# First group's 32x32 solve on VectorE, the bias table in four parts, up projections on GpSimd's queue

## The chip, the cores and the metric

The kernel runs on one core of one Trainium2 chip. A core has TensorE (PE in the profile: matmuls, with PEld for its weight loads), VectorE (DVE), ScalarE (ACT), GpSimd (POOL) and SyncE (SP, which here only issues DMAs). Each engine works through its own instructions in a fixed order and waits on semaphores; DMAs are issued from the queues of SyncE, ScalarE and GpSimd. The metric is the device time of one execution in microseconds. Before the change the median of three runs is 2808.73 us (2807.68 to 2812.29).

## The reference

Two transformer blocks of 256 tokens and width 2048, one after the other, all in float32. The change concerns only the first half of the first block:

```python
def first_block(x, ...):
    u = rms_norm(x, norm1_g)
    proj = u @ w_in                       # 2048 x 6432
    q, k, v, z = split(proj, ...)
    attn = dilated_attention(q, k, v, rel_bias_table)   # 16 heads of 64
    rw = rwkv7_time_mix(z, ...)                         # 16 heads of 64
    h = x + concat([attn, rw]) @ w_out
    h = h + (silu(gate) * up) @ w_down    # feed-forward, 5632
    return rms_norm(h, final_g)

def rwkv7_step(state, inp):               # scanned over the 256 tokens
    r, w, k, v, a, bb = inp
    sa = einsum('bhij,bhj->bhi', state, a)
    state = state * w + sa * bb + v * k   # outer products per head
    return state, einsum('bhij,bhj->bhi', state, r)

def reference(x, ...):
    return second_block(first_block(x, ...), mem_2, ...)
```

The attention's bias depends on the distance of query and key alone: `bias_table[t5_bucket(...)]`, 32 buckets by 16 heads. The second block (three attentions, a gated merge, a convolution and a feed-forward) is left as it is.

## The kernel before

Every large product is a call of `lin` (lines 344 to 399). A weight matrix lies packed in blocks of up to 512 columns; for each pair of k-tiles SyncE loads a `raw` tile (line 376), ScalarE rounds it to `wh` (line 385), VectorE subtracts to get the rest `wl` (line 386), and TensorE runs three matmuls for each k-tile and each half of the tokens (line 394): high by high, high by low, low by high. The tiles come from rings, three `raw`, three `wh`, two `wl`, and after the first block a second ring is made on the memory that its tiles give up. So TensorE can be ahead of VectorE and ScalarE by a few tiles only.

`block1_mix` runs the projections of the first block in a fixed list and, between their k-tiles, a set of tasks written as generators: `tick` adds the matmuls' modelled nanoseconds to a program clock and steps each task whose due time has come; a `yield 4000.0` puts the task to sleep for so much of that clock. The program order that results is the order in which each engine gets its instructions, except that weight loads and splits are pulled ahead by a priority (`LOAD_AHEAD`, `SPLIT_AHEAD`). The tasks are:

- `rwkv`: for each of four groups of four heads, `rwkv_pre` and `rwkv_group`. The scan over tokens is done in chunks of 32, eight in a group. `rwkv_group` makes the 32x32 blocks D of all chunks (VectorE masks them, line 621), stores them with two DMAs to `scN` (line 626), transposes v into UV, and calls `solve_T`. That loads N back from `scN` (four DMAs, line 654), loads an identity into T (line 657), and inverts the triangular blocks by 31 steps of a multiplication (line 662) and an addition (line 664), 62 small operations, each of which needs the one ahead of it. T goes to `scT` (line 666).
- `chains`: for each group the recurrence over eight chunks, from `load_solved` (T back as `TTx`, line 674) through `chain`: in each chunk matmuls `ch` on TensorE (line 727), with small copies on VectorE and ScalarE between them (`Xc`, `UV`, `Ux`, `S`, `Y`, lines 699 to 721). After a chain `rwkv_out` does the group norm (lines 735 to 743), a transpose `yt`, the gate `g` and the scaling `rw`, and splits the result into `mixh` and `mixl`.
- `attention`: quarters of four heads; `attn_load` brings `L`, the bias of two heads at a time laid out by query and key (line 883), q, k and v.

The bias comes from `attn_consts`: a matmul looks up all distances, VectorE copies the row `brow`, GpSimd stores it to `biasd` (line 786) and two DMAs write the table `toepd` (16 heads x 128 x 384) from it with a shifted start for each query (line 791). `load_up` loads the up projections `lup` of a group with two DMAs (line 521).

The last projection of the block is w_out in four blocks of 512 columns. As long as tasks are left, `block1_mix` runs passes over its first 14 of 16 k-tiles into spools `wa`; `block1_out` then does the blocks without a pass in full, and the rest with the last two k-tiles, adding `wa`.

## Time and profile before

| | before |
|---|---|
| median of three runs | 2808.73 us |
| profiled execution | 2810.79 us |
| its span, first to last instruction | 2808.8 us |
| mean granted TensorE clock | 0.996 |
| TensorE busy | 2763.9 us, 98% |
| VectorE busy | 1741.4 us, 62% |
| ScalarE busy | 1551.5 us, 55% |
| GpSimd busy | 167.2 us, 6% |
| HBM read | 518.46 MB |

A row of a timeline reads: start in us, duration in us, engine, line, operation, what it writes and reads, how often, and in brackets the idle time of the engine ahead of it and what ended it. A row of the windows has each engine's busy time with its count of instructions, then the granted clock, the share of time in which the DMA engines were busy, and GB/s. A row of the waits has the total, the number and the longest. Lines are those of the kernel before. Buffer numbers are left out of names.

### The profile page before, as it was taken

The page shows a single profiled execution, that of the slowest core. Times are in us where ns is not written, and L with a number is a line of the kernel's source. Part 1 is how long each engine was busy: PE and PEld are TensorE (multiplying, and loading weights), DVE is VectorE, ACT ScalarE, POOL GpSimd, SP SyncE. Part 2 cuts the span into 40 slices and gives each one's busy share as a digit, 9 for nine tenths or more (in the row PEclk, how much of TensorE's full clock was granted, in tenths as well). Part 3 has the DMA queues.
Part 4 walks back from the last instruction along what each step waited for, and adds up shares of the span by engine and source line. Part 5 has one row for each costly group of instructions (what it writes and reads, how often), then busy time and mean ns, then how long its engine had stood idle before and what let it go on. Part 6 is the DMA issues. An engine that isn't in the chain of part 4 may idle for free.

```text
span 2808.8 us, 40012 instructions
## 1 busy us (share of the span) xinstructions
PE 2763.9 (98%) x13496; PEld 2313.9 (82%) x13496; DVE 1741.4 (62%) x3121; ACT 1551.5 (55%) x2847; POOL 167.2 (6%) x380
## 2 busy tenths in 40 slices
PE   7989999999999999999999999999999999999999
PEld 7878888878888888888888888888888888888887
DVE  5666777675555555555756666665667676766554
ACT  6545556555455454444655755555556666666444
POOL 2432404000000000000000000000000000000000
PEclk9999999999999999999999999999999999999999
DMA  8555557766666666666754556666555555555665
GB/s 250 183 160 183 187 177 220 229 200 186 189 192 188 189 190 191 188 192 190 222 184 155 161 175 200 200 201 196 186 187 185 187 180 187 186 185 186 202 201 166
DMA packets 163910, 534.76 MB, mean 190 GB/s; under 512 B 18993, under 2 KB 29879, under 8 KB 163704
## 3 DMA queue, kind: packets, MB, share of 16 engines
q1 hardware_dynamic: 149644, 503.24, 57.0%
q10 hardware_dynamic: 9516, 16.27, 1.7%
q0 software_dynamic: 4544, 12.69, 1.6%
q8 instruction: 106, 1.74, 0.3%
q14 instruction: 100, 0.82, 0.1%
HBM read 518.46 MB, written 16.82 MB: 191 GB/s over the span
## 4 chain that ended last, share of the span: by engine, by line
PE 91%; DMA 4%; POOL 2%; DVE 1%; ACT 1%; issue 1%; SPq 0%; DVEq 0%; ACTq 0%; POOLq 0%
PE lin L394 84%; PE ch L727 2%; PE tr L263 1%; DMA toepd<-biasd 1%; PE uT L263 1%; POOL T L664 1%; DVE wl L386 1%; POOL X L662 0%; PE D L257 0%; PE o L257 0%; DMA raw<-in_w_in_dram 0%; ACT wh L385 0%; PE pt L257 0%; PE lg L257 0%; ACT junk L293 0%
## 5 line engine op out<-in xcount | busy, mean ns | idle before, releaser
L386 DVE TENSOR_TENSOR wl<-raw,wh 128x512 fp32r<-128x512 f32 (+2 forms) x1848 | 1267.4, 688 | 853.3 <-PE lin L394 758.2
L385 ACT CAST wh<-raw 128x512 fp32r<-128x512 f32 (+2 forms) x1848 | 1140.1, 619 | 1080.5 <-PE lin L394 1014.1
L394 PE MATMUL lin<-wl,x2h 128*128 128x512 f32 (+2 forms) x800 | 295.0, 369 | 3.8 <-DVE wl L386 3.8
L394 PE MATMUL lin<-wh,x2l 128*128 128x512 f32 (+2 forms) x800 | 291.2, 365 | 0.0
L394 PE MATMUL lin<-wl,u2h 128*128 128x512 f32 x704 | 281.0, 399 | 0.0
L394 PE MATMUL lin<-wl,hhi 128*128 128x512 f32 x704 | 275.0, 391 | 0.0
L394 PE MATMUL lin<-wh,u2l 128*128 128x512 f32 x704 | 274.6, 390 | 0.0
L394 PE MATMUL lin<-wl,uh 128*128 128x512 f32 x704 | 274.0, 391 | 0.0
L394 PE MATMUL lin<-wh,hlo 128*128 128x512 f32 x704 | 274.0, 389 | 0.0
L394 PE MATMUL lin<-wh,ul 128*128 128x512 f32 x704 | 272.3, 390 | 0.6 <-DVE ul L330 0.6
L394 PE MATMUL lin<-wh,x2h 128*128 128x512 f32 (+2 forms) x800 | 248.1, 366 | 0.1
L394 PE MATMUL lin<-wh,uh 128*128 128x512 f32 x704 | 228.1, 391 | 0.6 <-ACT uh L329 0.6
L394 PE MATMUL lin<-wh,u2h 128*128 128x512 f32 x704 | 225.5, 392 | 0.0
L394 PE MATMUL lin<-wh,hhi 128*128 128x512 f32 x704 | 220.0, 389 | 0.0
L394 PE MATMUL lin<-wl,xh 128*128 128x512 f32 (+2 forms) x512 | 192.2, 376 | 6.6 <-DVE wl L386 6.4
L394 PE MATMUL lin<-wh,xl 128*128 128x512 f32 (+2 forms) x512 | 178.5, 349 | 0.0
L394 PEld LDWEIGHTS lin<-wl,x2h 128*128 128x128 f32 x800 | 151.2, 189 | 30.2 <-DVE wl L386 7.2
L394 PEld LDWEIGHTS lin<-wh,x2h 128*128 128x128 f32 x800 | 149.9, 189 | 25.4 <-ACT wh L385 1.2
L394 PEld LDWEIGHTS lin<-wh,x2l 128*128 128x128 f32 x800 | 151.2, 189 | 22.9
L394 PE MATMUL lin<-wh,xh 128*128 128x512 f32 (+2 forms) x512 | 156.6, 354 | 11.7 <-ACT wh L385 11.7
L394 PEld LDWEIGHTS lin<-wh,uh 128*128 128x128 f32 x704 | 132.1, 188 | 28.7 <-ACT uh L329 1.5
L394 PEld LDWEIGHTS lin<-wh,u2h 128*128 128x128 f32 x704 | 132.1, 188 | 28.0
(426 smaller groups left out, 3735.6 us busy)
## 6 DMA issues: line engine op xcount, KB each, us to landing
raw<-in_w_in_dram SPq DMA_DIRECT2D x268, 512.0 KB, 3.7
raw<-in_w_gate_up_dram SPq DMA_DIRECT2D x176, 512.0 KB, 3.9
raw<-in_w_down_dram SPq DMA_DIRECT2D x176, 512.0 KB, 3.6
raw<-in_w_up_dram SPq DMA_DIRECT2D x176, 512.0 KB, 3.8
raw<-in_w_out_dram SPq DMA_DIRECT2D x64, 512.0 KB, 3.8
raw<-in_w_mem_kv_dram SPq DMA_DIRECT2D x16, 512.0 KB, 4.3
raw<-in_w_br_fox_dram SPq DMA_DIRECT2D x12, 512.0 KB, 4.3
raw<-in_w_br_sb_dram SPq DMA_DIRECT2D x12, 512.0 KB, 4.4
```

The costliest lines, as they stand in the source:

```text
L263: self.nc.tensor.transpose(out, in_, self.ident[p0:p0 + n, p0:p0 + n])
L385: nc.scalar.copy(wh[:, :m * n], raw[:, cs])
L386: nc.vector.tensor_tensor(wl[:, :m * n], raw[:, cs], wh[:, :m * n].bitcast(F32), op=ALU.subtract)
L394: self.nc.tensor.matmul(ps[tb], lhsT=x, rhs=w, start=k == first and i == 0 and not (one and tb), stop=k == last - 1 and i == 2, skip_group ...
L664: gp.tensor_tensor(w, w, x, op=ALU.add)
L727: self.nc.tensor.matmul(out, lhsT=lhsT, rhs=rhs, start=start, stop=True, skip_group_check=True)
```

## The change

The 62 operations of group 0's solve go from GpSimd to VectorE; groups 1 to 3 keep GpSimd. The loads of N and of the identity move into `load_N`, called right behind the two stores of D; the transposes of v come after them, and the solve is put into the program 13 us of program clock behind the loads. Since VectorE's weight splits can be pulled ahead of it by their priority, `hold` makes a 1x1 copy from the latest `wl` into a tile, which ties the tile's first use to that place among the weights. The time at which a solve counts as done becomes the clock plus 48 us (30 us for group 0).

The table is made in four tensors of four heads, each with its own hold, store and two writes, 10 us of program clock apart, and the task starts after block 4 of w_in instead of ahead of it. `lup` of groups 1 to 3 is loaded from GpSimd's queue.

```diff
--- before.py
+++ after.py
@@ -386,6 +386,7 @@
                     nc.vector.tensor_tensor(wl[:, :m * n], raw[:, cs], wh[:, :m * n].bitcast(F32), op=ALU.subtract)
                 for tb in range(2):
                     for j in range(m):
+                        self.at = wl
                         k = k0 + j0 + j
                         kx = k if kmap is None else kmap(k)
                         h, l = (t[:, j * n:(j + 1) * n] for t in (wh, wl))
@@ -401,6 +402,10 @@
 
     SPLIT_AHEAD = 0
     LOAD_AHEAD = 500
+
+    def hold(self, t):
+
+        self.nc.vector.tensor_copy(t, self.at[t.base_partition():t.base_partition() + 1, 0:1].bitcast(F32))
 
 
 class Block1(Builder):
@@ -518,7 +523,7 @@
         nc, cs = self.nc, slice(S * g, S * g + S)
         for i in range(2):
             r = slice(64 * i, 64 * i + 64)
-            nc.sync.dma_start(self.lup[r, i, :], self.A["lup"][r, cs])
+            (nc.gpsimd if g else nc.sync).dma_start(self.lup[r, i, :], self.A["lup"][r, cs])
 
     def rwkv_pre(self, g):
 
@@ -602,13 +607,6 @@
                 r = slice(64 * hh, 64 * hh + 64)
                 o = 64 * x + 32 * hh
                 v.tensor_tensor(BK[r, :, o:o + 32], c32(src)[r], st.linv[r], op=ALU.mult)
-        yield 1500.0
-        yield from wait("v")
-        st.v = self.mixed_T(nat[2], 2, st, self.slot([P, 2, S], "v"))
-
-        for p in range(2):
-            v.scalar_tensor_tensor(r_[:, p, :], r_[:, p, :], self.pv("r_k", 2 * st.g + p), k[:, p, :],
-                                   op0=ALU.mult, op1=ALU.mult)
         yield 4500.0
         st.D, st.BKT, st.UV = self.set2("D", [P, 16, P]), self.set2("BKT", [P, 16, P]), self.set2("UV", [P, 16, 64])
         for p in range(2):
@@ -625,6 +623,14 @@
         for hh in range(2):
             nc.gpsimd.dma_start(self.scN[hh].rearrange("c t s -> t c s"),
                                 st.D[32 * hh:32 * hh + 32, :, 32 * hh:32 * hh + 32])
+        self.load_N(st)
+        yield from wait("v")
+        st.v = self.mixed_T(nat[2], 2, st, self.slot([P, 2, S], "v"))
+
+        for p in range(2):
+            v.scalar_tensor_tensor(r_[:, p, :], r_[:, p, :], self.pv("r_k", 2 * st.g + p), k[:, p, :],
+                                   op0=ALU.mult, op1=ALU.mult)
+        yield 3000.0
         nc.gpsimd.memset(st.UV[0:64], 0.0)
         pv = self.aux("V")
         for i in range(4):
@@ -637,11 +643,22 @@
                     v.tensor_copy(dst, src[:, hh])
                 else:
                     nc.scalar.copy(dst, src[:, hh])
-        self.solve_T(st)
         yield 1300.0
         ps = self.aux("bn")
         self.mm(ps, self.same, r_.rearrange("p a s -> p (a s)"))
         v.tensor_tensor(r_, st.v, ps.rearrange("p (a s) -> p a s", a=2), op=ALU.mult)
+        yield max(0.0, st.sent + 13000.0 - self.clock)
+        self.solve_T(st)
+
+    def load_N(self, st):
+
+        gp = self.nc.gpsimd
+        st.N = self.p1.tile([P, 32, 32], F32, tag="N", name=self.nm("N"))
+        for q in range(4):
+            gp.dma_start(st.N[32 * q:32 * q + 32], self.scN.rearrange("h c t s -> (h c) t s"))
+        st.T = self.p1.tile([P, 8, 32], F32, tag="T", name=self.nm("T"))
+        gp.dma_start(st.T, self.A["c_eye4"].rearrange("p (a b) -> p a b", a=8))
+        st.sent = self.clock
 
     def solve_T(self, st):
 
@@ -649,23 +666,21 @@
 
         nc = self.nc
         gp = nc.gpsimd
-        N = self.p1.tile([P, 32, 32], F32, tag="N", name=self.nm("N"))
-        for q in range(4):
-            gp.dma_start(N[32 * q:32 * q + 32], self.scN.rearrange("h c t s -> (h c) t s"))
-        T = self.p1.tile([P, 8, 32], F32, tag="T", name=self.nm("T"))
+        N, T = st.N, st.T
         X = self.p1.tile([P, 256], F32, tag="X", name=self.nm("X"))
-        gp.dma_start(T, self.A["c_eye4"].rearrange("p (a b) -> p a b", a=8))
+        eng = gp if st.g else nc.vector
+        if not st.g:
+            self.hold(X[0:1, 0:1])
         for u in range(31):
             m, n = u // 4 + 1, 31 - u
             x = X[:, :m * n].rearrange("p (a b) -> p a b", a=m)
             w = T[:, 0:m, u + 1:32]
-            gp.tensor_tensor(x, T[:, 0:m, u:u + 1].to_broadcast([P, m, n]),
-                             N[:, u:u + 1, u + 1:32].to_broadcast([P, m, n]), op=ALU.mult)
-            gp.tensor_tensor(w, w, x, op=ALU.add)
+            eng.tensor_tensor(x, T[:, 0:m, u:u + 1].to_broadcast([P, m, n]),
+                              N[:, u:u + 1, u + 1:32].to_broadcast([P, m, n]), op=ALU.mult)
+            eng.tensor_tensor(w, w, x, op=ALU.add)
         for q in range(4):
             gp.dma_start(self.scT[st.g % 2].rearrange("h c t s -> (h c) t s")[:, q::4, :], T[32 * q:32 * q + 32])
-        self.solved = max(self.solved, self.clock + 14000.0) + 62000.0
-        st.solved = self.solved
+        st.solved = self.clock + (48000.0 if st.g else 30000.0)
 
     def load_solved(self, st):
         for p in range(2):
@@ -696,6 +711,8 @@
             for p in range(2):
                 self.acc(xy[p], D[:, 8 * p + c, :], UV[p], start=(c == 0 and p == 0))
             X = self.p1.tile([P, 64], F32, tag="Xc", name=self.nm("Xc"), bufs=2)
+            if c == 0:
+                self.hold(X[0:1, 0:1])
             v.tensor_copy(X[0:64], xy[0][0:64])
             nc.scalar.copy(X[64:128], xy[1][0:64])
             yield 4000.0 if c == 0 else 1300.0
@@ -782,13 +799,19 @@
         self.mm(ps[0:16, :], tab, oh)
         row = self.aq("brow")[0:16]
         nc.vector.tensor_copy(row, ps[0:16, :])
-        b = self.drp.tile([16, 512], F32, tag="biasd", name="biasd")
-        nc.gpsimd.dma_start(b, row)
-
-        self.toepd = self.drp.tile([16, P, 384], F32, tag="toepd", name="toepd")
-        for c0, w, e in ((0, 256, 127), (256, 128, 255)):
-            ap = bass.AP(tensor=b.tensor, offset=b.offset + e, ap=[[512, 16], [-1, P], [1, w]])
-            nc.gpsimd.dma_start(self.toepd[:, :, c0:c0 + w], ap)
+
+
+        self.toepd = []
+        for a in range(4):
+            self.hold(row[0:1, 511:512])
+            b = self.drp.tile([16, 512], F32, tag=f"biasd{a}", name=f"biasd{a}")
+            nc.gpsimd.dma_start(b, row)
+            t = self.drp.tile([4, P, 384], F32, tag=f"toepd{a}", name=f"toepd{a}")
+            for c0, w, e in ((0, 256, 127), (256, 128, 255)):
+                ap = bass.AP(tensor=b.tensor, offset=b.offset + 2048 * a + e, ap=[[512, 4], [-1, P], [1, w]])
+                nc.gpsimd.dma_start(t[:, :, c0:c0 + w], ap)
+            self.toepd.append(t)
+            yield 10000.0
 
     def aq(self, name, w=512):
         return self.p1.tile([P, w], F32, tag="aq%d" % w, name=self.nm(name), bufs={512: self.NAQ, 768: self.NAL}[w])
@@ -879,8 +902,9 @@
         Ls, nat = [], []
         for h2 in range(2):
             Ls.append(q2(self.aq("L", 768)))
-            h0 = 4 * a + 2 * h2
-            self.nc.sync.dma_start(Ls[-1], self.toepd[h0:h0 + 2].rearrange("h q j -> q h j"))
+            if not a:
+                self.hold(Ls[-1][0:1, 0, 0:1])
+            self.nc.sync.dma_start(Ls[-1], self.toepd[a][2 * h2:2 * h2 + 2].rearrange("h q j -> q h j"))
         for n, sp in zip("qkv", spools):
             nat.append(q2(self.aq("n" + n)))
             self.nc.sync.dma_start(nat[-1], sp[2][:, :, cs])
...
@@ -1196,10 +1219,11 @@
             for i in range(3):
                 self.lin("w_in", 1 + i, xT, self.nat_evac(z[i], rs))
                 have.add("krv"[i])
-            self.attn_consts()
-            self.start(attention())
             for i in range(3):
                 self.lin("w_in", 4 + i, xT, sp[i][0](rs))
+                if not i:
+                    self.start(self.attn_consts())
+                    self.start(attention())
             have.add("0 stored")
 
             def attention_in(a):
```

Where the order moves, first on SyncE among the first loads of w_in (`raw` is a weight tile, `L` the bias of two heads). Before:

```order
39 L521 DMA lup<-in_lup_dram 64x256 [waits DMAHW4_49,DMAHW2_49,PE_49]
40 L376 DMA raw_720<-in_w_in_dram 128x1024 [waits DMAHW3_49,DVE_49]
41 L376 DMA raw_754<-in_w_in_dram 128x1024 [waits DMAHW6_49,DVE_49]
42 L521 DMA lup<-in_lup_dram 64x256 [waits DMAHW5_49,PE_49]
43 L376 DMA raw_791<-in_w_in_dram 128x1024 [waits DMAHW7_49,DVE_49]
44 L376 DMA raw_825<-in_w_in_dram 128x1024 [waits DMAHW3_49,DVE_49]
45 L376 DMA raw_871<-in_w_in_dram 128x1024 [waits DMAHW4_49,DMAHW0_49,DVE_49]
46 L883 DMA L_3351<-toepd 128x2x384 [waits DMAHW1_49,DMASW4_49,DMASW3_49]
47 L883 DMA L_3353<-toepd 128x2x384 [waits DMAHW2_49]
48 L376 DMA raw_905<-in_w_in_dram 128x1024 [waits DMAHW6_49,DVE_49]
```

and now:

```order
39 L376 DMA raw_720<-in_w_in_dram 128x1024 [waits DMAHW2_49,DVE_49]
40 L376 DMA raw_754<-in_w_in_dram 128x1024 [waits DMAHW6_49,DMAHW3_49,DVE_49]
41 L376 DMA raw_791<-in_w_in_dram 128x1024 [waits DMAHW7_49,DMAHW4_49,DVE_49]
42 L376 DMA raw_825<-in_w_in_dram 128x1024 [waits DMAHW5_49,DMAHW2_49,DVE_49]
43 L376 DMA raw_871<-in_w_in_dram 128x1024 [waits DMAHW3_49,DVE_49]
44 L376 DMA raw_905<-in_w_in_dram 128x1024 [waits DMAHW4_49,DVE_49]
45 L376 DMA raw_964<-in_w_in_dram 128x1024 [waits DMAHW5_49,DMAHW0_49,DVE_49]
46 L376 DMA raw_998<-in_w_in_dram 128x1024 [waits DMAHW6_49,DMAHW1_49,DVE_49]
```

Between the weights stand neither the `lup` loads nor the two loads of L; the first L comes at row 118.

On VectorE the place at which group 0's solve begins in the kernel as changed (`X` and `T` are its tiles, `wl` a weight split, `UV` the transposed v); before, these rows of X and T stand on GpSimd:

```order
150 L386 TENSOR_TENSOR wl_1426<-raw_1393,wh_1425 128x512 [waits DVE_49,PE_49]
151 L643 COPY UV_1118<-V_1412 32x4x64 [waits Activation_49]
152 L386 TENSOR_TENSOR wl_1447<-raw_1444,wh_1446 128x512 [waits DVE_49,DMAHW4_49,PE_49,Activation_49]
153 L643 COPY UV_1118<-V_1412 32x4x64 [waits Activation_49]
154 L408 COPY X_1462<-wl_1447 1x1 [waits DVE_49]
155 L408 COPY brow_1175<-wl_1447 1x1 [waits DMASW1_49]
156 L678 TENSOR_TENSOR X_1462<-T_1264,N_1259 128x31 [waits DMASW4_49,DMASW3_49,DMASW5_49,DMASW2_49,DVE_49]
157 L680 TENSOR_TENSOR T_1264<-T_1264,X_1462 128x31 [waits DVE_49]
158 L643 COPY UV_1118<-V_1412 32x4x64 [waits Activation_49]
```

The first multiplication waits for the loads of N. Up to row 284, its last addition, 28 weight splits stand between the solve's rows. On GpSimd the stores of D stand behind the first part of the table:

```order
44 L808 DMA biasd_1178<-brow_1175 16x512 [waits DVE_49]
45 L812 DMA toepd_1180<-biasd_1178 512x1x256 [waits DMASW4_49]
46 L812 DMA toepd_1180<-biasd_1178 512x1x128
47 L624 DMA scN<-D_1116 32x16x32 [waits DVE_49]
48 L624 DMA scN<-D_1116 32x16x32 [waits DMASW0_49]
49 L808 DMA biasd_1319<-brow_1175 16x512 [waits DMASW1_49,DVE_49]
50 L658 DMA N_1259<-scN 32x1024 [waits DMASW7_49,DMASW2_49,DMASW0_49]
51 L658 DMA N_1259<-scN 32x1024 [waits DMASW3_49]
52 L658 DMA N_1259<-scN 32x1024
53 L658 DMA N_1259<-scN 32x1024 [waits DMASW5_49]
54 L812 DMA toepd_1321<-biasd_1319 512x1x256 [waits DMASW6_49,DMASW1_49]
```

On TensorE the end of group 3's recurrence (`ch` is the chain, `yt` the transposes, `g` the gate, `lin` the projections). Before, some rows of it:

```order
2534 L727 MATMUL ch_5456<-Xc_6061,TTx 128x64 [waits Activation_49]
2535 L394 MATMUL lin_6216<-wl_6221,mixh_5479 128x512 [waits DVE_49]
2536 L394 MATMUL lin_6216<-wh_6220,mixl_5480 128x512
2537 L394 MATMUL lin_6216<-wh_6230,mixh_5479 128x512 [waits Activation_49]
2538 L394 MATMUL lin_6217<-wh_6220,mixh_5479 128x512 [waits Activation_49]
2539 L394 MATMUL lin_6217<-wl_6221,mixh_5479 128x512
...
2546 L394 MATMUL lin_6216<-wh_6260,mixh_5479 128x512 [waits Activation_49]
2547 L394 MATMUL lin_6217<-wh_6260,mixh_5479 128x512
2548 L727 MATMUL ch_5456<-Ux_389,D_4389 128x64 [waits DVE_49]
2549 L727 MATMUL ch_5456<-Ux_389,D_4389 128x64
2550 L394 MATMUL lin_6216<-wl_6261,mixh_5479 128x512 [waits DVE_49]
2551 L394 MATMUL lin_6216<-wh_6260,mixl_5480 128x512
```

and now:

```order
2480 L395 MATMUL lin_6120<-wh_6146,mixh_5617 128x512 [waits Activation_49]
2481 L395 MATMUL lin_6121<-wh_6146,mixh_5617 128x512
2482 L744 MATMUL ch_4990<-Xc_5592,TTx 128x64 [waits Activation_49]
2483 L744 MATMUL ch_4990<-UV_4001,BKT_4000 128x64 [waits DVE_49]
...
2485 L744 MATMUL ch_4990<-Ux_388,D_3999 128x64 x2
2486 L744 MATMUL ch_4990<-S_5691,ARx_383 128x64 [waits DVE_49,Activation_49]
...
2489 L744 MATMUL ch_4990<-Xc_5711,TTx 128x64 [waits Activation_49]
2490 L744 MATMUL ch_4990<-Ux_389,D_3999 128x64 [waits DVE_49]
...
2492 L263 MATMUL yt_5940<-k_c_ident,Y_4989 128x128 [waits DVE_49,PE_49]
...
2494 L263 MATMUL yt_5940<-k_c_ident,Y_4989 128x128 [waits Activation_49]
2495 L257 MATMUL g_5941<-gT,gup 128x256 [waits DMAHW0_49,PE_49]
...
2498 L395 MATMUL lin_6120<-wl_6147,mixh_5617 128x512 [waits DVE_49]
```

In the rows of before, projections stand between TTx and Ux·D, and 58 more behind that up to the transposes; now the rows from the first TTx to the gate follow each other, and the projection behind them waits for VectorE. Before, four passes into `wa` are made and block1_out has four short ends; now there are two passes, two full blocks and two short ends.

More of the change, by code (lines that the diff above doesn't have):

```diff
@@ L1133, in block1_mix @@
             have = self.have = set()
-            self.solved = 0.0
             groups = []
```

## The prediction

> **What bounds the kernel now.** I read the profiled page first (part 1, engines), then busy time by windows over the first 620 us, since every edited line runs there, then the engine queues' waits and the chain of waits.
>
> ```profile
> span 2808.8 us, 40012 instructions
> PE 2763.9 (98%) x13496; PEld 2313.9 (82%) x13496; DVE 1741.4 (62%) x3121; ACT 1551.5 (55%) x2847; POOL 167.2 (6%) x380
> ...
> core 0: us, PE busy (x) PEld busy (x) DVE busy (x) ACT busy (x) POOL busy (x), PEclk, DMA share, GB/s
> 42.00:66.00 24.00, 19.51 (x141) 18.17 (x141) 14.34 (x32) 11.72 (x24) 1.44 (x2) 0.93 0.90 242
> 66.00:81.00 15.00, 12.05 (x96) 11.22 (x94) 11.97 (x23) 6.46 (x13) 0.00 (x0) 1.00 0.59 193
> 150.00:160.00 10.00, 4.83 (x14) 3.99 (x15) 3.19 (x6) 2.49 (x6) 1.15 (x3) 0.55 0.26 69
> 590.00:620.00 30.00, 25.47 (x99) 18.87 (x99) 23.01 (x37) 18.24 (x42) 0.56 (x1) 0.89 0.58 180
> ```
>
> TensorE is busy 98% of the span, and the change neither adds nor removes a projection matmul (line 394). So the time moves only by TensorE idle time, and by stretches at half clock (PEclk well under 1). The four windows show where idle time is to be won: 4.49 us of 24, 2.95 of 15, 5.17 of 10, 4.53 of 30. All other idle time of the first 620 us is small.
>
> The causes, in the chain of waits (first row), SyncE's waits, and the GpSimd and TensorE timelines:
>
> ```profile
> 42.41 22.97 DMA toepd<-biasd
> ...
> SPq L883 <- DMA toepd<-biasd: 8.4, 1, 8.4
> SPq L521 <- PE lora L257: 6.7, 3, 3.1
> ...
> 97.94 1.30 POOL L626 DMA_DIRECT2D scN<-D  x2 [54.50 <-DVE D L621]
> 103.51 1.98 POOL L654 DMA_DIRECT2D N<-scN  x4 [4.26 <-DMA scN<-D]
> 110.10 0.51 POOL L662 TENSOR_TENSOR X<-T,N 128x31 f32<-128x31 f32 x1 [4.48 <-DMA N<-scN]
> ...
> 142.61 2.35 POOL L666 DMA_DIRECT2D scT<-T  x4 [0.30 <-POOL T L664]
> ...
> 155.17 0.66 PE L727 MATMUL ch<-Xc,TTx 128*128 128x64 f32 x2 [6.94 <-DMA TTx<-scT]
> ...
> 159.47 0.63 PE L394 MATMUL lin<-wh,xl 128*128 128x512 f32 x1
> 159.90 0.63 PE L394 MATMUL lin<-wl,xh 128*128 128x512 f32 x1
> ...
> 161.57 0.40 PE L394 MATMUL lin<-wh,xl 128*128 128x512 f32 x1
> 161.80 0.40 PE L394 MATMUL lin<-wl,xh 128*128 128x512 f32 x1
> ```
>
> The bias table's transfer takes 22.97 us while the DMA engines are 0.90 busy, and SyncE stands 8.4 us on it with weight loads queued behind. Group 0's chain then needs 12.2 us from D to the solve (97.94 to 110.10), 32.5 us of solve, 12.6 us to TTx in place; TensorE waits 6.94 us. After that stop matmuls start 0.43 us apart until about 161.2, and 0.23 apart later: 6.0 us at half rate, 3.0 us lost.
>
> **The change part by part.** The sum goes against the profiled execution, 2810.79 us, which is 2.06 above the median 2808.73; its span of 2808.8 leaves 2 us outside, which nothing here touches.
>
> *A, the bias table in parts, and the up projections off SyncE.* Removed: idle 4.49 + 2.95 = 7.4 us, and 0.07 x 24 = 1.7 us by clock, 9.1 in all. SyncE's order no longer has a table load between early weights, nor the `lup` loads on which it stood 6.7 us. About 1 us should stay (an evacuation wait or two). The same bytes are still moved: a quarter takes about 22.97/4 = 5.7 us, 10 us of program apart, beside weight loads. Nothing shows a quarter alone, so its bounds are 0 (the ring covers it) and 5.7 for one quarter that is wholly uncovered; I take 1.5, since the whole table cost 7.4 with SyncE blocked as well. A = -9.1 + 1 + 1.5 = -6.6, bounds -9 to -2.4.
>
> *B, the first wait on TTx.* Removed: 6.94 + 3.0 = 9.9 us. The order shows the chain's first TTx matmul 133 rows later on TensorE (row 957 for 824). Between the last solve row and that matmul lie about 11.6 us of matmuls (by 0.23 us each), against the 12.6 of the rows above: a new wait of about 1, bounds 0 to 4; 0.7 is taken. B = -9.2.
>
> *C, the solve on VectorE.* 62 small operations join VectorE, with 28 weight splits among them. No row shows a solve operation there; the nearest are these, of three answers of the groups by form:
>
> ```profile
> L276 DVE TENSOR_TENSOR gn<-gn 128x8 f32<-128x8 f32 x3 | 0.5, 159 | 0.0
> ...
> L386 DVE TENSOR_TENSOR wl<-raw,wh 128x512 fp32r<-128x512 f32 x20 | 14.1, 711 | 7.6 <-PE lin L394 3.4 <-ACT wh L385 1.2 <-ACT linv L534 1.2
> ...
> L386 DVE TENSOR_TENSOR wl<-raw,wh 128x512 fp32r<-128x512 f32 x22 | 15.2, 689 | 9.0 <-PE lin L394 8.0 <-ACT wh L385 0.6 <-issue 0.4
> ```
>
> From 159 ns for 8 elements and 0.29 us for 128 (the row of S at 569.76 in the fence of part D) comes about 150 + 1.1 ns an element; a solve operation has 50 on average, so 0.21 us each and 13 us together. Adding such prices for all 133 VectorE rows of that stretch (the splits at 0.69) gives 51 us; with independent neighbours overlapped by 0.08 us (in the fence of part D a split starts 0.61 after a row of 0.69, at 581.60), 44. TensorE has 28 x 6 projection matmuls at 0.23 there and 5 us of others, 43. So the stretch costs between nothing and 8 us; I take 2.5, nearer the low end, as the small operations stand between splits on which they do not depend. Less 0.4: while GpSimd solves, a split takes 711 ns instead of 689 (the last two rows, us 110 to 142 and 224 to 260), 22 ns x 20.
>
> [...]
>
> C = +2.1, bounds 0 to 8.
>
> *D, the recurrence's end stands bare.* The program now makes two early w_out passes instead of four (the loop stops as soon as no task is left), and in the new TensorE order the last two chain steps, the transposes yt and the g matmuls stand together, with no projection between them; the next one needs a split that VectorE has behind the group norm. Before, projections lay between all of these. Its price from the rows of before, where each hop shows:
>
> ```profile
> 565.40 0.33 PE L727 MATMUL ch<-Xc,TTx 128*128 128x64 f32 x2
> 566.48 0.23 DVE L707 COPY Ux<-ch 64x64 f32<-64x64 f32 x1 [0.49 <-ACT Ux L706]
> 568.39 0.55 PE L727 MATMUL ch<-UV,BKT 128*128 128x64 f32 x4
> 569.76 0.29 DVE L718 TENSOR_TENSOR S<-S,lamC 128x128 f32<-128x128 f32 x1
> 572.04 0.55 PE L727 MATMUL ch<-S,ARx 128*128 128x64 f32 x4
> 573.33 0.20 ACT L700 COPY Xc<-ch 64x64 f32<-64x64 f32 x1 [0.89 <-DVE Xc L699]
> 578.70 0.55 PE L727 MATMUL ch<-Ux,D 128*128 128x64 f32 x4
> 579.29 0.26 ACT L721 COPY Y<-ch 64x128 f32<-64x128 f32 x1 [0.23 <-PE ch L727]
> 580.99 0.69 DVE L737 TENSOR_TENSOR Y<-Y,gnm 128x512 f32<-128x512 f32 x1
> 581.60 0.69 DVE L386 TENSOR_TENSOR wl<-raw,wh 128x512 fp32r<-128x512 f32 x1
> 582.17 0.63 ACT L739 ACTIVATE gq<-Y 128x512 f32<-128x512 f32 x1
> 585.15 0.17 DVE L286 TENSOR_SCALAR gn<-gnv 128x8 f32<-128x8 f32 x1
> 585.35 0.17 DVE L273 TENSOR_SCALAR gn<-gn 128x8 int32<-128x8 int32 x1
> 592.78 0.60 PE L263 MATMUL yt<-k_c_ident,Y 128*128 128x128 f32 x4
> 593.21 1.89 PE L257 MATMUL g<-gT,gup 128*128 128x256 f32 x8
> 594.96 0.41 DVE L761 TENSOR_SCALAR rw<-rw,k_pv 128x256 f32<-128x256 f32 x1 [0.36 <-ACT rw L759]
> 597.51 0.62 ACT L1248 CAST mixh<-rw 128x512 fp32r<-128x512 f32 x1
> 598.16 0.69 DVE L1249 TENSOR_TENSOR mixl<-rw,mixh 128x512 fp32r<-128x512 f32 x1
> ```
>
> TTx to Ux 1.31 us (565.40 to 566.71), BKT to S 1.66 (568.39 to 570.05), S·ARx to Xc 1.49 (572.04 to 573.53), TTx to Ux again 1.31, Ux·D to Y 0.85 (578.70 to 579.55): 6.6. Group norm: three 128x512 operations and one more for the mean at 0.69, the square 0.63, one scalar and ten to eleven small ones about 0.2 apart: some 6.0 with the wide ones overlapping a little. From yt to the second scaling 2.6 (592.78 to 595.37), then two at 0.69, mixh 0.62, mixl 0.69 and the split 0.69: 3.4. Sum 18.6, with handovers about 19.2. TensorE works about 4.2 of it (g 1.89, yt 0.60, ten short rows of the chain), work that it has anyway: 15.0 idle. Work in it at half clock 0.4, and after it the 3.0 of the first stop: D = +18.4. Bounds 14 (no clock loss, hops a little shorter since no split is in their way) and 21 (weight loads must refill as well).
>
> *E, the end of the first block.* Us 590 to 620 lose 4.53 us idle and 0.11 x 30 = 3.3 by clock, 7.8, around the four short passes of two k-tiles each and their additions to h. Now two such passes stand at the end, behind two full ones whose weights are at hand. I take back more than half, E = -4.5, bounds -6 to -2.
>
> *F, group 3.* Its first TTx comes earlier in TensorE's order by some 7.7 us of matmuls, and its solve is GpSimd's as before. D to TTx takes 97.94 to 155.17 = 57.2 us in the rows of group 0 and I count about 57 us of matmuls in between: +0.5, bounds 0 to 2. The eleven holds (1x1 copies) cost nothing on TensorE: 11 x 0.16 us of VectorE, which is 62% busy.
>
> Sum: -6.6 - 9.2 + 2.1 + 18.4 - 4.5 + 0.5 = +0.7, so 2811.5 in a profiled execution and **2809.4** for the median: gains and losses of some 20 us that cancel. Less than 0.2% either way (2803.1 to 2814.3) is no change that a measurement of this kernel tells.
>
> **The rivals.**
>
> *R1, slower: N comes late and VectorE waits in order.* The first solve operation stands in VectorE's order in front of the splits, so it decides from the point at which N lands more than about 13 us behind D. Before, 12.2 were needed with nothing else in GpSimd's queue. Now part one of the table is issued ahead of scN and part two between N and what follows: 5.7 us of table in front of a 4.3 us scN. For it: the table ran at a 0.90 DMA share. Against it: scN is 10 us of program behind part one. A delay of 5 us stalls the splits, TensorE after two tiles, and lets the clock fall once: 5 - 1 + 3.0 = +7, so 2816.4.
>
> *R2, slower: VectorE becomes the bound of the solve's stretch.* C's stretch at 8 instead of 2.5: 2814.9. It decides if the operations do not overlap: for it, dependent small rows start 0.20 us apart for 0.17 of work (585.15 and 585.35); against it stands the overlap used in C.
>
> *R3, faster: the end is covered better than its order shows.* D at 14 and C at 0, A at -8.6: -3.9 us - 2.1 - 2.0 gives 2800.9. For it: hops in an idle machine have no split in their way. Against it: TensorE's order is fixed, and the norm's rows are one dependent chain.
>
> *R4, the early solve isn't what removes the wait.* TTx stands 133 rows later in any case, and 6.94 us are fewer than the 22 us of matmul work in these 133 rows. The time is that of the forecast; only the reason differs.
>
> **How the numbers follow.** Forecast, with R4 inside it, 0.44; R1 0.17, R2 0.12; R3 0.27. The forecast's own range is A, B, C, D, E at their bounds taken as independent: about 7 us to either side, 2803 to 2816. R3 reaches below it and R1 above, so the range is 2799 to 2820. Faster 0.28, same 0.43, slower 0.29.
>
> **What would show it.** In the profile of the changed kernel: A, windows 42:66 and 66:81 with TensorE busy over 23 and 14.5 us, and no SyncE wait on the table of over 1 us. B, no wait of TensorE on TTx over 2 us around us 140 to 180. C, the waits of lin on wl in the solve's 43 us in sum under 4 us; R2 shows as more, spread evenly, R1 as one wait on DMA N at the first solve row. D, one stretch near us 580 to 610 of about 19 us in which TensorE is busy about 4, behind it 6 us at half clock; if the projections fill it, the forecast is wrong by up to 18 us on the fast side. E, the last 30 us of the block with under 3 us idle. What would make it wrong most is D's size, then the table's quarters meeting the loads of N.

## The result and the profile after

The changed kernel takes 2823.55 us (median of four runs, 2821.7 to 2824.87) against 2808.57 us before (median of four as well): ratio 1.0052, 95% interval 1.0040 to 1.0065, 15 us slower. The forecast was 2809.4 us, its range 2799 to 2820. The profiled execution took 2823.22 us, its span is 2821.5 us.

The windows of TensorE in the first 640 us, before and then after (length, TensorE busy with its instructions, granted clock, DMA share, GB/s):

```profile
40.00:90.00 50.00, 42.56 (x326) 0.97 0.72 202
90.00:135.00 45.00, 43.35 (x317) 1.00 0.61 188
135.00:180.00 45.00, 38.06 (x193) 0.89 0.49 148
330.00:415.00 85.00, 84.18 (x488) 1.00 0.58 181
415.00:520.00 105.00, 101.11 (x575) 1.00 0.72 226
520.00:640.00 120.00, 115.47 (x556) 0.97 0.64 205
```

```profile
40.00:90.00 50.00, 48.50 (x400) 1.00 0.52 154
90.00:135.00 45.00, 38.34 (x247) 0.92 0.75 223
135.00:180.00 45.00, 43.48 (x220) 1.00 0.61 186
330.00:415.00 85.00, 83.39 (x484) 0.98 0.57 182
415.00:520.00 105.00, 97.90 (x536) 0.95 0.71 220
520.00:640.00 120.00, 106.19 (x500) 0.93 0.54 167
```

From these a ledger can be kept. What TensorE loses in a stretch is its idle time, plus half of its busy time in those parts of the stretch in which the clock is granted at half (in us 338.6 to 342.0 of the changed kernel it was 0.50 and matmuls of 128x512 started 0.43 us apart, 0.23 behind that). (Multiplying the whole window by the missing clock would count idle time twice.) In us:

| stretch | before | after | difference | forecast |
|---|---|---|---|---|
| 0 to 40 | 10.4 | 11.9 | +1.5 | 0 |
| 40 to 90 | 9.2 | 1.5 | -7.7 | -8.1 (A without its contention) |
| 90 to 180 | 11.6 | 11.2 | -0.4 | -5.6 (A's contention +1.5, B -9.2, C +2.1) |
| 180 to 330 | 1.3 | 0.7 | -0.6 | 0 |
| 330 to 415 | 0.8 | 3.3 | +2.5 | 0 |
| 415 to 520 | 3.9 | 11.2 | +7.3 | +0.5 (F, which was placed here) |
| 520 to 640 | 7.6 | 18.5 | +10.9 | +13.9 (D and E) |
| 640 to 2790 | 5.6 | 5.3 | -0.4 | 0 |
| sum | 50.3 | 63.6 | +13.3 | +0.7 |

The spans differ by 12.7 us. Behind us 2790, mostly behind its last matmul, TensorE is idle 4.0 us before and 5.1 after, which would make the sum +14.4. So the ledger accounts for the result to within 2 us. Other runs agree less closely: over whole profiles, span less loss lies between 2749.8 and 2754.6 us, so a difference of two ledgers is good to some 5 us at worst. The early stalls went, the wait on TTx went, the bare end came, all three near the size that was forecast. Two places are new: 90 to 135 and 330 to 520.

**Us 90 to 135.** The timelines of GpSimd, VectorE and TensorE in the changed kernel:

```profile
103.33 2.21 POOL L812 DMA_DIRECT2D toepd<-biasd  x2 [0.27 <-issue]
...
107.45 0.51 POOL L808 DMA_DIRECT2D biasd<-brow  x1 [1.78 <-DVE brow L408]
118.13 2.18 POOL L812 DMA_DIRECT2D toepd<-biasd  x2 [10.16 <-DMA biasd<-brow]
120.30 0.56 POOL L526 DMA_DIRECT2D lup<-in_lup_dram  x1
120.84 0.16 POOL L544 MEMSET lam<- 128x16 f32 x1
...
108.58 0.19 DVE L678 TENSOR_TENSOR X<-T,N 128x31 f32<-128x31 f32 x1 [1.43 <-DMA N<-scN]
...
114.97 0.68 DVE L542 SCALAR_TENSOR_TENSOR linv<-sg,linv 128x512 f32<-128x512 f32 x1
121.03 0.71 DVE L547 TENSOR_TENSOR_SCAN lam<-lam,first 128x264 f32<-128x264 f32 x1 [5.37 <-POOL lam L544]
...
118.06 0.44 PE L263 MATMUL zt<-k_c_ident,kA 128*128 128x128 f32 x2 [2.16 <-DMA kA<-sp_kA]
...
124.29 0.80 PE L395 MATMUL lin<-wl,xh 128*128 128x512 f32 x1 [4.18 <-DVE wl L386]
```

Read from below: TensorE waits 4.18 us for a weight split. VectorE couldn't make it, since ahead of it in its order stands a scan that waits 5.37 us for a 0.16 us memset of `lam`. GpSimd couldn't make that, since ahead of it in its order stands part three of the table, which waits 10.16 us for a small store of `brow`, which is slow behind the transfer of part two. The solve's own loads were nearly in time: its first row waited 1.43 us for N.

How slow, three rows show, from issue to landing: part two's two writes, that store (16x512), and the load of kA, for which TensorE waits 2.16 us:

```profile
DMA to landing us min/median/max: 12.8/13.0/13.2
...
DMA to landing us min/median/max: 10.4/10.4/10.4
...
DMA to landing us min/median/max: 7.1/7.1/7.1
```

Part two landed at 117.65, the store at 117.84, kA at 118.02. From the first issue to the last landing the four parts took 13.7, 14.3, 11.1 and 14.8 us, the whole table in the kernel before 24.0 (us 41.37 to 65.38). So a part took far more than a quarter of the whole's time, and 10 us of program clock behind it the next store still met it. The load of kA took 3.1 us in the kernel before.

**The end of the recurrence.** TensorE's waits in us 555 to 600 of the changed kernel (total, times, longest):

```profile
PE yt L263 <- DVE Y L760: 6.7, 1, 6.7
PE lin L395 <- DVE wl L386: 2.8, 1, 2.8
PE ch L744 <- DVE Ux L724: 2.1, 2, 1.0
PE ch L744 <- DVE S L735: 0.8, 1, 0.8
PE ch L744 <- ACT Xc L717: 0.6, 1, 0.6
```

That is the bare end as the order showed it: 13.0 us of idle time where the forecast had 15.0, and 4.7 by clock where it had 3.4.

### The profile page after: what moved, and what is told of

The parts are those of the page before. It is cut to its first block, busy times and chain, and to the rows that moved or that the text cites. A ratio compares the mean times of both kernels' runs of the same rounds, so it can differ in the third digit from the quotient of the medians.

```text
span 2821.5 us, 40043 instructions
## 1 busy us (share of the span) xinstructions
PE 2768.0 (98%) x13496; PEld 2317.7 (82%) x13496; DVE 1749.2 (62%) x3192; ACT 1550.5 (55%) x2843; POOL 146.7 (5%) x331
## 5 line engine op out<-in xcount | busy, mean ns | idle before, releaser
L395 PE MATMUL lin<-wh,xh 128*128 128x512 f32 (+2 forms) x512 | 159.5, 357 | 10.5 <-ACT wh L385 10.4
```

The source lines that it names most:

```text
L395: self.nc.tensor.matmul(ps[tb], lhsT=x, rhs=w, start=k == first and i == 0 and not (one and tb), stop=k == last - 1 and i == 2, skip_group ...
```

## The experiments

Theory T: the loss is made of the bare end and of GpSimd's small memsets behind the table's parts. Rival U: the 62 operations that VectorE got are what costs. Ratios are to the kernel before on the same chip, with 95% intervals.

**Four passes.** The pass loop without its stop:

```diff
             for c in range(4):
-                if not self.tasks:
-                    break
                 self.wa.append(self.spool(f"wa{c}"))
```

> The changed kernel, but always with four early w_out passes, as before the change (the loop's stop is left out). Theory T (the loss is the bare end of the recurrence, 13.0 us idle and about 7 us by half clock in us 555 to 600 of the changed kernel, plus waits on small GpSimd memsets): the end is covered again by the passes, about 18 us come back, of which 2 to 4 are paid again for the four short ends: 2806 to 2810 us. Rival U (the work that the solve puts on VectorE is what costs, spread over the first 200 us): 2820 us or more.

Measured 2808.43 us, 1.0003 (0.9993 to 1.0012): 0.0049 less than the changed kernel, 13.8 us. In us 520 to 640 the ledger falls from 18.5 to 6.4 us. The windows' row of this run for the stretch:

```profile
520.00:640.00 120.00, 115.27 (x554) 0.99 0.65 208
```

So the bare end, net of the short passes, is worth about what D and E together said (13.9): 13.8 us by the times, 12.0 by the ledger.

**Memsets on VectorE.**

```diff
         for t in (st.lam, lv):
-            nc.gpsimd.memset(t[:, :, 0:1], 0.0)
+            nc.vector.memset(t[:, :, 0:1], 0.0)
```

> The changed kernel with one edit: the two small memsets of lam and linv in each group are VectorE's instead of GpSimd's. In the changed kernel VectorE's scan waits 5.4 us (group 1) and 3.0 us (group 3) for such a memset, which stands in GpSimd's order behind the bias table's transfers and a solve. Theory T: the stop of 4.2 us at us 124 and the one of 1.6 us at us 336 go, with the half clock behind them, 6 to 9 us: 2815 to 2818 us; TensorE's 2.2 us wait on kA stays. Rival U: no more than 2 us, 2821 to 2824.

Measured 2813.19 us, 1.0023 (1.0013 to 1.0032): 0.0029 less than the changed kernel, 8 us. The scan goes through at once while GpSimd stands on the store as before:

```profile
106.06 0.51 POOL L808 DMA_DIRECT2D biasd<-brow  x1 [1.92 <-DVE brow L408]
117.05 2.18 POOL L812 DMA_DIRECT2D toepd<-biasd  x2 [10.47 <-DMA biasd<-brow]
...
114.31 0.70 DVE L547 TENSOR_TENSOR_SCAN lam<-lam,first 128x264 f32<-128x264 f32 x1
```

TensorE's wait on kA stays (2.3 us), and the stop near us 336 is gone, where the scan of group 3 had waited 3.0 us for a memset behind a solve.

**Both.**

> The changed kernel with both edits, four early w_out passes and the memsets on VectorE. Theory T: the two gains add up, 2797 to 2803 us, faster than the kernel before. Rival V (what is won at one place is waited for at the next, since the loads or the chain set the time): no better than the better of the two alone, 2806 or more.

Measured 2801.83 us, 0.9981 (0.9972 to 0.9990). The gains nearly add up, 0.0071 for 0.0049 + 0.0029.

**Group 0's solve back on GpSimd, all else as changed.**

```diff
-        eng = gp if st.g else nc.vector
-        if not st.g:
-            self.hold(X[0:1, 0:1])
+        eng = gp
```

> The changed kernel with group 0's solve back on GpSimd, and all else as changed (loads of N early, table in parts, two passes). Theory T: the solve's place matters little in itself; the end stays bare and the memset of lam now stands behind a solve as well: 2820 to 2830 us. Rival U (VectorE's 62 operations are the cause): 2808 to 2814 us.

Measured 2817.02 us, 1.0035 (1.0022 to 1.0047). It lies between the bounds that T and U gave, some 5 us under the changed kernel, so neither number is right. The profile has the bare end (16.6 us lost in 555 to 600) and the stop at us 126 (5.06 us) as before, and no wait on TTx, though GpSimd solves. So VectorE is not needed to take that wait away; the early loads and the new due times do it (the table's part alone, below, leaves it). This bears out R4 of the prediction. Nor are the 5 us the price of the operations on VectorE: in the solve's own stretch, 90 to 180, this run loses 13.6 us to the changed kernel's 11.2. By the ledgers it gains in 330 to 520 (9.8 for 14.5).

**The parts of the change alone.** The three parts of the diff, each by itself in the kernel before:

> The kernel before with the table in four parts alone (its holds, the later start of its task, the loads of L from the parts); the solve and the up projections as before, and four early w_out passes. Theory T: the early stalls go (6 to 8 us), the wait on TTx stays in part since GpSimd still solves, and the memset of lam may be late on GpSimd: ratio 0.997 to 1.000 of before, 2799 to 2807 us. Rival W (the parts cost as much at us 115 as the whole table cost at us 42 to 81): 1.000 or more.

> The kernel before with the solve's part alone (VectorE for group 0, early loads of N, the new times at which a solve counts as done); one table and up projections on SyncE as before. Its program makes two w_out passes, so this part alone brings the bare end. Theory T: minus 10 for TTx, plus about 18 for the bare end, minus 4 at the end of the block: ratio 1.001 to 1.003, 2811 to 2816 us. Rival U (the solve's move is a gain in itself and the loss is the table's and the queue's): 0.998 or less.

> The kernel before with the up projections of groups 1 to 3 on GpSimd's queue alone. Theory T: SyncE no longer stands 6.7 us on the matmuls of the group before, but the weights that it loads were not what TensorE waited for: 0.999 to 1.001. Rival Z (these two loads held up the early weights): 0.998 or less.

| part alone | median, us | ratio | interval |
|---|---|---|---|
| table in parts, later start | 2818.16 | 1.0035 | 1.0021 to 1.0049 |
| solve on VectorE | 2809.50 | 1.0000 | 0.9990 to 1.0009 |
| up projections on GpSimd's queue | 2818.11 | 1.0031 | 1.0019 to 1.0043 |

TensorE's windows of the table's part alone, and then of the solve's part alone:

```profile
40.00:90.00 50.00, 48.40 (x399) 1.00 0.51 156
90.00:135.00 45.00, 40.43 (x258) 0.92 0.77 226
135.00:180.00 45.00, 37.14 (x189) 0.92 0.51 152
```

```profile
40.00:90.00 50.00, 42.71 (x335) 1.00 0.73 204
135.00:180.00 45.00, 44.40 (x231) 1.00 0.61 188
520.00:640.00 120.00, 107.20 (x498) 0.94 0.55 171
```

The table's part takes the early stalls away (7.4 us idle to 1.6) and puts 4.6 us idle and 3.1 by clock into 90 to 135, beside a wait on TTx that stays (6.35 us). Of the idle time 3.8 us are for kA, which landed 9.5 us after its issue; the memset of lam stands ahead of the wait here, so the transfer alone does this. Further on the run loses 7.0 us in 415 to 520 (3.9 before) and 13.1 in 520 to 640 (7.6 before). Theory T had this part as a gain. Rival W had the direction, but its reason covers only the first place, 6.0 us for the 7.5 that went; what makes the part a loss comes at the two later ones, and the cause of the last was not looked for. The solve's part takes the wait on TTx away and brings the bare end in the same move, because the shorter time at which a solve counts as done ends the tasks after two passes: zero in sum. That was not expected: T had 1.001 to 1.003, and the forecast's B, D and E add up to +4.7. By the ledger 9.3 us went in 135 to 180 and only 9.0 came in 520 to 640 (16.6 for 7.6), where D and E had 13.9. With four passes it is the gain that it could be:

> As the run with the solve's part alone, with four w_out passes always. Theory T: the bare end is covered, TTx isn't waited for, the early table stalls stay: ratio 0.996 to 0.998, 2796 to 2802 us. If it is not faster than before, the wait on TTx has only moved.

Measured 2797.93 us, 0.9966 (0.9953 to 0.9979).

The third part came out as neither theory had it. By the ledger that run loses 3.1 us more than the kernel before in 40 to 90, 2.3 less in 135 to 180, and 7.0 more in 520 to 640, far behind the loads, with waits for `mixh` at us 526 (2.3 us) and 606 (3.1). To see if any shift of the order costs so much, one due time in the kernel before was moved:

```diff
             def rwkv():
-                yield 4000.0
+                yield 7000.0
                 self.lora_lo(lo)
```

> The kernel before with one due time changed: the first task sleeps 7 us of program clock instead of 4 before its first step. No work, queue or engine changes, only the places of tasks among the weights. Theory S (a few tenths of a per cent hang on where the tasks fall, without any cause in the edit itself): a move of 0.1% to 0.4% either way, in stops that lie 100 us and more behind the shifted step. Rival R (the order is robust, so a move of 0.3% must have its cause in the queue): 0.999 to 1.001.

Measured 2808.36 us, 1.0001 (0.9992 to 1.0011), though TensorE's order differs from before in hundreds of rows. So a shift alone need not cost. And in the changed kernel and in a better one (the run with parts further apart, four passes and the memsets on VectorE, below) the queue of the up projections makes no difference that the times show:

> The changed kernel with the up projections back on SyncE's queue, two w_out passes, memsets on GpSimd. Theory T (GpSimd's memset waits behind the table's parts, with or without the up projections): the stop near us 124 stays, 1.003 to 1.006. Rival Z (the third part of the change alone costs the 0.3% that it cost in the kernel before): 1.002 or less.

> The best version so far (four passes, memsets on VectorE, parts 25 us apart; 0.9956 of before) with the up projections on SyncE. Theory S (the 0.3% of the up projections in the kernel before is a change of order far downstream, not the queue): within 0.1% of that version, 0.9945 to 0.9967, either way. Rival Z (GpSimd's queue costs): 0.9935 or less.

Measured 1.0048 (1.0031 to 1.0065) beside 1.0052, and 0.9961 (0.9947 to 0.9974) beside 0.9956. Why this part alone costs 0.3% in the kernel before stays open; it is no cause of the changed kernel's loss.

**Parts further apart.**

```diff
-            yield 10000.0
+            yield 25000.0
```

> The changed kernel with 25 us of program clock instead of 10 between the table's four parts, so that the store of one row no longer waits behind the part ahead of it; two passes, memsets on GpSimd. Theory T (the memset of lam is late because GpSimd stands 10 us on the third row's store behind the second part's transfer): the stops at us 118 and 124 shrink by 4 to 8 us with their clock, ratio 1.002 to 1.004. Rival X (the memset waits for the up projections' place or the scheduler's order, not for the table): no change, 1.005.

Measured 2819.28 us, 1.0039 (1.0024 to 1.0054). In us 90 to 135 the loss falls from 9.7 to 2.3 us, as T said; but 2.2 us come back at us 190, where another memset of lam stands on GpSimd behind the wait for group 1's N. Two things differ at the first place, not one: no part is in flight when the second part's store is issued, which lands in 4.1 us, and the memset now stands ahead of that store's wait in GpSimd's order. With this edit, four passes and the memsets on VectorE:

> The changed kernel with four w_out passes, the memsets of lam and linv on VectorE, and 25 us of program clock between the table's parts. Theory T (the waits at us 116 to 124 come from parts one and two of the table standing close together with the loads of kA): against the run with the first two edits alone (0.998 of before) TensorE's wait on kA of 2.2 us and the 1.7 us of half clock behind it go: 0.996 to 0.997, 2796 to 2800 us. Rival X (kA is late whatever the table does, or a part now collides with the next group's N): 0.998 or more.

Measured 2796.75 us, 0.9956 (0.9941 to 0.9971).

**The table whole, and early.** Two runs, both with four passes and the memsets on VectorE, show what the table's part is worth once the rest is mended: the whole table at the later place, and the table as before.

```diff
...
+        b = self.drp.tile([16, 512], F32, tag="biasd", name="biasd")
+        nc.gpsimd.dma_start(b, row)
+        t = self.drp.tile([16, P, 384], F32, tag="toepd", name="toepd")
+        for c0, w, e in ((0, 256, 127), (256, 128, 255)):
+            ap = bass.AP(tensor=b.tensor, offset=b.offset + e, ap=[[512, 16], [-1, P], [1, w]])
+            nc.gpsimd.dma_start(t[:, :, c0:c0 + w], ap)
+        self.toepd = [t[4 * a:4 * a + 4] for a in range(4)]
...
```

> The changed kernel with four w_out passes and the memsets on VectorE, but the table again as one tensor written by two DMAs, at the later place (behind block 4 of w_in). Theory T (what counts is how many bytes of table are in flight beside the loads of N and kA): N lands some 10 us later, VectorE stands at the first solve row and TensorE behind it: 1.000 to 1.004, 2808 to 2819 us. Rival Y (the later place alone is what removes the early stalls, and the split into parts is worth nothing): 0.997 to 0.999, as with the parts.

> The kernel before with the solve's part, the up projections on GpSimd, four w_out passes and the memsets on VectorE, and the table as before, early and whole. So it differs from the changed kernel with four passes and VectorE memsets (0.998) by the table alone. Theory T (the parts take 9 us of early loss away and put 4 to 6 back at us 116 to 124): 0.999 to 1.000, unless the parts cost more than the early table: then 0.996 to 0.997, and the table's part of the change is a loss.

Measured 2802.38 us, 0.9978 (0.9968 to 0.9987), and 2798.24 us, 0.9958 (0.9941 to 0.9974). The first loses 9.6 us in 90 to 135. As T had it N is 9 us late, VectorE's first solve row stands at 117.80 instead of 108.58:

```profile
117.80 0.19 DVE L678 TENSOR_TENSOR X<-T,N 128x31 f32<-128x31 f32 x1 [2.07 <-DMA N<-scN]
```

But VectorE waits only 2.1 us for it, since its own splits are late as well (ScalarE waits 5.4 us for weights in 95 to 125), and the whole is no slower than four parts 10 us apart (0.9981). So T's 1.000 was wrong, Rival Y had the number, and at 10 us the split is worth nothing that these runs can tell. The second is faster than the parts at 10 us, 0.0023: the table's part of the change, as made and with its later start, is a loss of some 6 us even with all else mended (the two intervals just touch).

**The start.** In every run with the later start of the table's and the attention's tasks TensorE loses 7 to 12 us in 415 to 520 (changed 11.2, table alone 7.0, one table 12.3, best 11.3), in every run with the early start 2 to 5 (before 3.9, solve alone 2.1, table as before 3.8, shifted 4.9). The last experiment has four passes, the memsets on VectorE and the parts 25 us apart, as the best so far, and starts both ahead of block 4 again:

```diff
+            self.start(self.attn_consts())
+            self.start(attention())
             for i in range(3):
                 self.lin("w_in", 4 + i, xT, sp[i][0](rs))
-                if not i:
-                    self.start(self.attn_consts())
-                    self.start(attention())
```

> The best version so far (four passes, memsets on VectorE, parts 25 us apart; 0.9956 of before), with the table's task and the attention's started ahead of block 4 of w_in, as before the change, instead of behind it. Theory L (the stops of TensorE in us 415 to 520, 11 us in that version against 4 in the kernel before, come from the attention's later start, which moves its tasks among the memory's loads): idle and half clock there in sum 5 us or less, 0.993 to 0.995. Rival M (they come from the table's parts or from the holds): 9 us or more there, 0.9955 or more.

Measured 2792.65 us, 0.9938 (0.9922 to 0.9955), 16 us faster than the kernel before. TensorE's windows of this run:

```profile
40.00:90.00 50.00, 48.48 (x403) 1.00 0.54 173
90.00:135.00 45.00, 43.58 (x282) 1.00 0.73 213
135.00:180.00 45.00, 42.67 (x220) 1.00 0.73 221
415.00:520.00 105.00, 103.13 (x569) 0.98 0.69 217
520.00:640.00 120.00, 114.84 (x532) 0.97 0.64 207
```

In 415 to 520 it loses 1.9 idle and 1.7 by clock, 3.6 for 11.3. So it is the later start, not the split or the holds (which of the two tasks, no run tells). What the start moves there, by the waits of ScalarE in the changed kernel (first row) and here (second), in us 415 to 520:

```profile
ACT memh L1298 <- DMA mem<-in_memT_dram: 6.2, 4, 2.6
```

```profile
ACT memh L1295 <- DMA mem<-in_memT_dram: 3.2, 3, 2.0
```

In the changed kernel the longest stop there is TensorE's, for the softmax of an attention quarter (`L`, on ScalarE), which stands behind such a load of the memory in ScalarE's order:

```profile
439.05 0.90 PE L263 MATMUL pt<-k_c_ident,L 128*128 128x128 f32 x3 [3.58 <-ACT L L859]
```

That the attention's last quarters fall among the memory's loads is an explanation that fits these rows and is not shown; what was tested is the start. Over other runs the waits of `memh` do not order the losses: the table's part alone has 2.5 us of them and loses 7.0 there, the up projections alone 4.1 and lose 3.4.

## Why the prediction was wrong

- **A, the early stalls: right in what went, mis-sized in what came.** Gone are 7.7 us (forecast 8.1). The term for the parts' contention, "I take 1.5", measured 8.1 us in 90 to 135 (9.7 lost against 1.6 before), beyond its bounds of 0 to 5.7. Two steps failed. First, "a quarter takes about 22.97/4 = 5.7 us": a part took 11 to 15, so it was still in flight when the next part's store and the load of kA were issued. Second, the wait was sought at N alone (R1), with the weight loads. What came late was kA (TensorE waits 2.2 us) and a memset in GpSimd's order behind a wait of part three (4.2 us), with 3.0 us by clock. That memset stands four rows behind the third part's store; the prediction went through what waits for the moved DMAs and not through all that is queued behind them. R1 came nearest in kind, a wait behind the parts with a price of 7, but N was waited for only 1.4 us.
- **B, the wait on TTx: right.** No wait of TensorE on TTx is left (forecast 0.7). R4, too: the run with the solve on GpSimd has none either.
- **C, the solve on VectorE: right as far as the rows show.** A solve operation takes 0.21 us in the median (forecast 0.21). TensorE is idle 1.5 us in all of 135 to 180, and its one long wait for a split in the solve's stretch is the memset's; R2 is out.
- **D and E, the bare end: right, and somewhat too large.** 13.9 forecast, 10.9 by the ledger, 13.8 by the run with four passes, 9.0 in the run with the solve's part alone.
- **F, later waits: wrong.** Only group 3's TTx was looked at, "+0.5", and the later start of the attention was put at nothing without a reason. From 330 to 520 the ledger has +9.8: 2.5 from a memset of lam behind a solve at us 334, and 7.3 in 415 to 520, the stretch in which the earlier start won 7.7 us in the best version. The prediction had not asked what else a task that starts one block later meets 300 us on.
- The 1.5 us more at the start of the span lie ahead of the change; the ledgers of all runs have 0 or about 1.7 by clock there, whatever the kernel.
- A slip without effect: R3 writes 3.9 us for D at 14, where 18.4 - 14 is 4.4; its 2800.9 is the sum with 4.4.

So the terms that were worked out from rows held, within 3 us each in the changed kernel. The two that were set small for want of a row (1.5 and 0.5) were together 16 us too low. In both, one named wait was followed, and not what else would meet the moved work.

## What to carry to other kernels

When DMAs with waits are moved into an engine's queue, list every instruction behind each of them in that engine's order, the tiny ones too: a 0.16 us memset behind a 10 us wait stopped three engines. Do not take a quarter of a transfer for a quarter of its time: here the parts took 11 to 15 us each, the whole 24. When a change shortens a task, look at what was hidden under its old length; here, with the solve's part alone, the two passes that fell away cost as much as the removed wait gave. Keep a ledger of idle time and half clock by stretch, which shows at once whether a part's gain went elsewhere, and try each part alone before judging the whole.

## What the runs showed of the hardware

Half clock came in pieces of 3.4, 6.8 and 13.7 us in the changed kernel's trace, and of 3.4, 6.8 and 10.2 us in that of the kernel before. One piece followed on short stops alone: the stretch around us 334 to 342 of the changed kernel has 1.6 us idle in all, its longest stop 1.09 us, and a piece of half clock begins at 338.6:

```profile
330.00:345.00 15.00, 13.39 (x72) 11.10 (x70) 9.70 (x20) 5.81 (x14) 12.79 (x31) 0.89 0.66 208
```

In the 3.4 us ahead of that piece TensorE was busy 1.8 us, so here a stretch that was only partly idle went ahead of half clock; what decides it, no run shows. At the bare end the half clock (two pieces in us 564 to 584, 17.1 us in sum) lay to a good part on idle time and cost 4.7 us, where its length would suggest 8.5.

The small store of `brow` took 10.4 us to land (107.45 to 117.84) while the second part of the table was written; with the parts 25 us apart and none in flight, the second part's store took 4.1, and GpSimd waited 3.76 us for it:

```profile
114.75 1.13 POOL L812 DMA_DIRECT2D toepd<-biasd  x1 [3.76 <-DMA biasd<-brow]
```
